# A decoder trunk's down projection by seven products per four blocks, woven into the up projection

## Chip, cores and metric

One Trainium2 chip, one core. The metric is the time of one execution on the device, in microseconds (us); the lower the better.

## The reference

One inference step of two decoder layers, d_model 1024, for 512 prompt tokens and 32 sample tokens (8 sequences of 4), which share all weights:

```python
x += W_out [ Retention(h) || DilatedAttention(h) ],  h = RMSNorm(x), one projection h @ W_in
x += ConvFFN(RMSNorm(x))

def conv_ffn(h, ctx, w_up_l, conv_w_l, conv_b_l, w_down_l):
    u = h @ w_up_l
    ext = concatenate([ctx, u], axis=1)
    c = conv_b_l
    for j in range(3):
        c = c + ext[:, j:j + T] * conv_w_l[j]
    g, val = c[..., :2816], c[..., 2816:]
    return (silu(g) * val) @ w_down_l, ext[:, -2:]
```

W_up is 1024 x 5632, W_down 2816 x 1024. The change leaves what is computed as it is.

## The kernel before

All activations lie with features on the 128 partitions and the 544 tokens along the free axis, as two halves of 272 (`HC`), each with 256 prompt and 16 sample tokens. x is eight tiles `x[n]`, one per 128 features.

**Products.** Every large product runs in three passes of split operands: a tile `t` is split into a high part (ACT copies it into the type fp32r) and a low part (DVE subtracts). Then high x high, high x low and low x high are summed in PSUM. `products` (line 1196) issues for one block of 128 rows of weights 3 passes x 2 halves = 6 matmuls of 272 columns. A main block (`add_block`, line 297) is one block of 128 output features: 8 such groups of 6 for an up block, 4 or 5 for a down block. Here one group of 6 is called a step. Main blocks go to a PSUM tile `ps` of two banks, of which there are two (`main_bank`, line 349). Weights arrive in halves of a block: `load_w` (line 306) issues a DMA into `raw` (six buffers) on SP's queue, six halves ahead; `split_w` (line 312) makes `wh` on ACT and `wl` on DVE, three halves ahead.

**Order.** Nothing is scheduled at run time. The program writes its instructions through `Engine` (line 94), whose `call` at line 112 is the line that every row of the profile names, so rows are told apart by their tiles. `Clock` keeps an estimated time for each engine; `Stream` (line 153) holds generators of side work (attention, conv, norms, splits) and, between two steps of main products, `pump` emits a piece of those whose operands should be ready by that estimate. Each engine then runs its own list in order. Smaller matmuls of side work go to four PSUM banks, `sec`.

**FFN** (`ffn`, line 1063). The 22 blocks of the hidden dimension are worked in groups of 5, 5, 4, 4, 4 (`GROUPS`, line 25). `add_up` puts for each j two up blocks (gate and value half); `conv` (line 1078) follows each: DVE scales `ps` into `u` (2 rows), POOL puts the context into u and copies the new context out, ACT and then DVE twice make the three-tap sum `c`, ACT applies silu to the gate's, DVE multiplies into `y` (2 rows), ACT and DVE split it into `yh` and `yl`. `add_down` puts eight main blocks per group, which multiply the group's `yh`, `yl` by W_down; `down` adds each result to `x[n]` on DVE. The order is up(0), up(1), down(0), up(2), down(1), ..., up(4), down(3), down(4). The last eight main blocks of the program run once per half of the tokens, so that their successive matmuls have other weights each time and one bank.

**Mixer** (`mixer`, line 882). 28 blocks of W_in with attention and retention as side work; POOL adds the two terms of the rotary embedding (`ka`, `qa`, `kr`, `qr`) and multiplies `qd`. Then eight blocks of W_out twice.

## Time and profile before

| | before |
|---|---|
| time, median of 3 runs | 1444.89 us (1444.69 to 1445.34) |
| the profiled execution's own time | 1444.82 us |
| its span, first to last instruction | 1443.0 us |
| mean granted clock of TensorE | 0.997 of full speed |
| busy PE, DVE, ACT, POOL | 99%, 66%, 40%, 12% of the span |
| mean DMA rate | 121 GB/s |

PE is TensorE's matmul, PEld its loading of weights, which overlaps; DVE is VectorE, ACT ScalarE, POOL GpSimd, SP the queue that issues all DMAs. In a time line the first number is the start in us from the span's start, the second the length, x2 two rows put together; a bracket gives the idle time before the row and what ended it. An instruction's length holds its tail, so two rows that follow each other overlap a little: the step from one start to the next is what a row costs its engine.

### The profile page before, as it was taken

Reading aid. Unit: us, or ns where it says so; the run is one execution under the profiler, and the core shown is the slowest. Engines: PE = TensorE matmul, PEld = TensorE weight load, DVE = VectorE, ACT = ScalarE, POOL = GpSimd, SP = SyncE. Lnnn points to the kernel's source line nnn. Section 1 sums busy time; section 2 is a strip of 40 time slices with the busy share of each in tenths; the row PEclk is TensorE's granted clock in tenths of the full one; section 3 lists DMA queues with packets and bytes.
Section 4 is the critical chain, followed back from the end, with each engine's and each line's share of the span. In section 5 each row is a group of like instructions: output and inputs, shape, how many; then the busy total and the mean of one; then the engine's idle time right before and its main releaser. Section 6 shows DMA issues by size and latency. Waiting matters only on the chain.

```text
span 1443.0 us, 29646 instructions
## 1 busy us (share of the span) xinstructions
PE 1423.1 (99%) x11634; PEld 1356.0 (94%) x11634; DVE 949.2 (66%) x1857; ACT 571.6 (40%) x1108; POOL 178.9 (12%) x553
## 2 busy tenths in 40 slices
PE   8999999999999999999999999999999999999997
PEld 8888788999999999999998878899999999999996
DVE  8876556588775565757678765566977647566665
ACT  4454333444443333424435442243444424333334
POOL 4212222000000000000022221120000000000003
PEclk9999999999999999999999999999999999999999
DMA  6315682433222222223322339722422232322231
GB/s 237 97 60 181 233 311 89 154 113 115 93 80 88 91 83 101 93 84 104 104 90 90 119 105 316 283 91 101 148 104 88 65 112 70 107 88 89 88 93 63
DMA packets 98635, 173.92 MB, mean 121 GB/s; under 512 B 11072, under 2 KB 21440, under 8 KB 98496
## 3 DMA queue, kind: packets, MB, share of 16 engines
q1 hardware_dynamic: 98496, 172.03, 35.3%
q8 instruction: 92, 1.51, 0.4%
q14 instruction: 47, 0.39, 0.1%
HBM read 159.77 MB, written 12.21 MB: 119 GB/s over the span
## 4 chain that ended last, share of the span: by engine, by line
PE 94%; DVE 3%; issue 1%; DMA 0%; ACT 0%; SPq 0%; DVEq 0%; POOL 0%; ACTq 0%
PE ps L112 82%; PE sec L112 12%; DVE wl L112 1%; DVE rb L112 1%; DMA x<-xin 0%; DVE p L112 0%; SPq L112 0%; DVE xl L112 0%; DVE ra L112 0%; DVE sq L112 0%; ACT xh L112 0%; DVE va L112 0%; POOL qa L112 0%; DVEq L1381 0%; DVE tmp L112 0%
## 5 line engine op out<-in xcount | busy, mean ns | idle before, releaser
L112 PE MATMUL ps<-xh,wh 128*128 128x272 f32 x2304 | 489.0, 294 | 1.4 <-ACT wh L112 1.1
L112 PE MATMUL ps<-xh,wl 128*128 128x272 f32 x2304 | 477.3, 289 | 0.7 <-DVE wl L112 0.7
L112 PE MATMUL ps<-xl,wh 128*128 128x272 f32 x2304 | 477.3, 289 | 0.0
L112 PEld LDWEIGHTS ps<-xh,wh 128*128 128x128 f32 x2304 | 361.2, 189 | 19.0 <-issue 14.7
L112 PEld LDWEIGHTS ps<-xh,wl 128*128 128x128 f32 x2304 | 362.3, 189 | 0.9 <-DVE wl L112 0.9
L112 PEld LDWEIGHTS ps<-xl,wh 128*128 128x128 f32 x2304 | 362.3, 189 | 0.0
L112 ACT ACTIVATE wh<-raw 128x512 fp32r<-128x512 f32 (+2 forms) x432 | 248.3, 598 | 172.0 <-PE ps L112 158.8
L112 DVE TENSOR_TENSOR wl<-raw,wh 128x512 fp32r<-128x512 f32 (+2 forms) x432 | 295.9, 703 | 18.7 <-ACT wh L112 17.9
L112 DVE SCALAR_TENSOR_TENSOR c<-u,taps,c 128x560 f32<-128x560 f32 x176 | 141.2, 802 | 89.0 <-ACT c L112 85.9
L112 ACT ACTIVATE c<-u,taps 128x560 f32<-128x560 f32 x88 | 75.5, 857 | 227.1 <-DVE u L112 223.7
L112 DVE TENSOR_TENSOR x<-x,ps 128x544 f32<-128x544 f32 (+1 forms) x120 | 81.7, 681 | 119.6 <-PE ps L112 119.2
L112 PE MATMUL ps<-yh,wh 128*128 128x272 f32 x704 | 150.9, 288 | 0.0
L112 PE MATMUL ps<-yh,wl 128*128 128x272 f32 x704 | 150.5, 288 | 0.0
L112 PE MATMUL ps<-yl,wh 128*128 128x272 f32 x704 | 150.4, 288 | 0.0
L112 DVE TENSOR_TENSOR u<-ps,rstd 128x512 f32<-128x512 f32 (+1 forms) x176 | 69.2, 435 | 80.5 <-PE ps L112 80.4
L112 PEld LDWEIGHTS ps<-yh,wh 128*128 128x128 f32 x704 | 112.3, 188 | 0.1
L112 PEld LDWEIGHTS ps<-yl,wh 128*128 128x128 f32 x704 | 112.2, 188 | 0.1
L112 PEld LDWEIGHTS ps<-yh,wl 128*128 128x128 f32 x704 | 112.3, 188 | 0.0
L112 POOL COPY last<-u 128x2 f32<-128x2 f32 (+1 forms) x176 | 28.2, 192 | 667.2 <-DVE u L112 630.3
L112 DVE TENSOR_TENSOR rb<-ps,rope 32x544 f32<-32x544 f32 (+1 forms) x96 | 69.2, 721 | 1.4
L112 ACT ACTIVATE yh<-y 128x544 fp32r<-128x544 f32 x44 | 29.0, 659 | 82.6 <-DVE y L112 82.6
L112 PE MATMUL ps<-ch,wh 128*128 128x272 f32 x256 | 53.4, 290 | 0.0
(147 smaller groups left out, 1343.3 us busy)
## 6 DMA issues: line engine op xcount, KB each, us to landing
raw<-w_up SPq DMA_DIRECT2D x176, 256.0 KB, 2.8
raw<-w_in SPq DMA_DIRECT2D x112, 256.0 KB, 3.9
kt<-kc SPq DMA_DIRECT2D x80, 256.0 KB, 5.2
vt<-vc SPq DMA_DIRECT2D x80, 256.0 KB, 5.2
raw<-w_down SPq DMA_DIRECT2D x48, 256.0 KB, 2.6
raw<-w_out SPq DMA_DIRECT2D x32, 256.0 KB, 2.7
raw<-w_down SPq DMA_DIRECT2D x32, 192.0 KB, 2.4
s<-s SPq DMA_DIRECT2D x16, 256.0 KB, 5.3
```

What stands on the lines that cost most here:

```text
L112: return f(*args, **kw)
```

## The change

Of the 22 hidden blocks the first 16, in four groups of four, are multiplied by W_down in another way; the groups are now 4, 4, 4, 4, 2, 4. A group's four blocks are taken as two pairs (a, b), and the eight output blocks as four pairs m. With the two halves of the tokens, each 2 x 2 block product of a pair takes seven products of half width instead of eight (Strassen's method in Winograd's form).

- `make_forms` takes the place of the split of y for these 16: per pair of blocks four subtractions of 272 on POOL (`fa`, `fb`), then splits into `hb`/`lb`, `h1`/`l1` and twice `fh`/`fl`.
- `Weave.prepare` loads for each m the four blocks of weights in one DMA (`uraw`, 512 KB), makes four sums on POOL (`sums`, 4 rows of 2 x 128) and splits (`ah`/`al` of 768, `sh`/`sl` twice 512). Each of these tiles has one buffer.
- `Weave.step` issues one of the products P1, P4, P6, P2, P5, P7, P3: 2 pairs x 3 passes = 6 matmuls of 272 columns into one `sec` bank. P1, P6, P5, P3 go on in one bank, which ACT copies out between them (`one`, `snap`); `after` adds the results to x[2m] and x[2m+1], on DVE (three rows of 272, one of 544) and POOL (one of 272, one of 544).
- `tick` runs after each step of the next group's up blocks, of which there are 64: from the 24th on it puts the 28 woven steps among the 40 that remain, a step when it is due and its operands should be ready by the estimate, at the latest so that all are through at the 64th.
- The groups of 2 and 4 at the end are multiplied as before. Weights are loaded and split by whole blocks of eight, or of two or four smaller blocks together (`shared`), three units ahead for the load and two for the split; 432 splits become 182. Some tiles of the mixer (`qpad`, `qdp`, `k3`, `v3`, `vs`, `vss`) take the buffers of the woven weights, and `bd` those of the pool of blocks.

```diff
-GROUPS = ((0, 5), (5, 10), (10, 14), (14, 18), (18, 22))
+GROUPS = ((0, 4), (4, 8), (8, 12), (12, 16), (16, 18), (18, 22))
+MP = KB // 2
+STEPS = (("P1", 0, 0), ("P4", 0, 2), ("P6", 1, 1), ("P2", 0, 1), ("P5", 1, 0), ("P7", 1, 2), ("P3", 1, 3))
+LEAD, AMONG = 24, 40
...
-    def add_block(src, nk, rhs, evac, pre=None):
+    def add_block(src, nk, rhs, evac, pre=None, weave=None, shared=(0, 1)):
         i = len(main)
-        parts = [(0, nk)] if nk <= 4 else [(0, (nk + 1) // 2), ((nk + 1) // 2, nk)]
...
+        at, count = shared
+        parts = [(0, nk)] if i > 1 else [(0, nk // 2), (nk // 2, nk)]
...
+        if at == 0:
+            for a, b in parts:
+                halves.append((i, a, a + count * (b - a)))
...
+    def make_forms(a, b, first, i, dst):
+        fa, fb = blk([128, 2, HC], F32, "fa"), blk([128, 2, HC], F32, "fb")
+        pool.tensor_sub(fa[:, 0], a[:, 1], a[:, 0])
+        pool.tensor_sub(fa[:, 1], b[:, 1], fa[:, 0])
+        pool.tensor_sub(fb[:, 0], b[:, 1], a[:, 1])
+        pool.tensor_sub(fb[:, 1], b[:, 0], fa[:, 1])
+        hb = blk([128, 2, HC], F32R, "hb")
+        act.activation(hb, b, AF.Copy)
+        act.activation(first[0][:, i], a[:, 0], AF.Copy)
+        yield EW("dve", first[0], hb)
+        lb = blk([128, 2, HC], F32R, "lb")
+        dve.tensor_sub(lb, b, hb.bitcast(F32))
+        dve.tensor_sub(first[1][:, i], a[:, 0], first[0][:, i].bitcast(F32))
+        dst["P1"] = first[0][:, i], first[1][:, i]
+        dst["P2"] = hb[:, 0], lb[:, 0]
+        dst["P3"] = hb[:, 1], lb[:, 1]
+        for f, one, two_ in ((fa, "P5", "P6"), (fb, "P7", "P4")):
+            yield EW("act", f)
+            h = blk([128, 2, HC], F32R, "fh")
+            act.activation(h, f, AF.Copy)
+            yield EW("dve", h)
+            l = blk([128, 2, HC], F32R, "fl")
+            dve.tensor_sub(l, f, h.bitcast(F32))
+            dst[one] = h[:, 0], l[:, 0]
+            dst[two_] = h[:, 1], l[:, 1]
...
+    class Weave:
...
+        def tick(self):
+            self.count += 1
+            if not self.todo:
+                return
+            left = len(self.todo)
+            if self.count >= LEAD + (7 * MP - left) * AMONG / (7 * MP):
+                if self.count + left >= LEAD + AMONG or self.ready(*self.todo[0]):
+                    self.step(*self.todo.pop(0))
+                    if not self.todo:
+                        self.end()
+
+        def ready(self, m, p, g, q):
+            if (m, g) not in self.weights or any(p not in self.forms(i) for i in range(self.nk)):
+                return False
+            aps = [*self.weights[m, g], *(t for i in range(self.nk) for t in self.forms(i)[p])]
+            return clock.when("pe", aps) <= clock.now["pe"]
+
+        def prepare(self):
+            for m in range(MP):
+                w = wpool.tile([128, self.nk, 4, 128], F32, name=name("uraw"), tag="uraw", bufs=1)
+                sp.dma_start(w, self.src[m])
+                yield EW("pool", w)
+                sums = wpool.tile([128, self.nk, 4, 128], F32, name=name("sums"), tag="sums", bufs=1)
+                pool.tensor_add(sums[:, :, 0], w[:, :, 3], w[:, :, 2])
+                pool.tensor_sub(sums[:, :, 1], sums[:, :, 0], w[:, :, 0])
+                yield EW("pool", w)
+                pool.tensor_sub(sums[:, :, 2], w[:, :, 0], w[:, :, 3])
+                pool.tensor_sub(sums[:, :, 3], w[:, :, 1], sums[:, :, 1])
+                yield IF(lambda: m == 0 or (m - 1, "P2") in self.seen)
+                yield EW("act", w)
+                ah, al = (wpool.tile([128, self.nk, 3, 128], F32R, name=name(n), tag=n, bufs=1) for n in ("ah", "al"))
+                act.activation(ah, w[:, :, 0:3], AF.Copy)
+                yield EW("dve", ah)
+                dve.tensor_sub(al, w[:, :, 0:3], ah.bitcast(F32))
+                self.weights[m, 0] = ah, al
+                yield IF(lambda: m == 0 or (m - 1, "P3") in self.seen)
+                sh, sl = (wpool.tile([128, self.nk, 4, 128], F32R, name=name(n), tag=n, bufs=1) for n in ("sh", "sl"))
+                for a in (slice(0, 2), slice(2, 4)):
+                    yield EW("act", sums)
+                    act.activation(sh[:, :, a], sums[:, :, a], AF.Copy)
+                    yield EW("dve", sh)
+                    dve.tensor_sub(sl[:, :, a], sums[:, :, a], sh[:, :, a].bitcast(F32))
+                self.weights[m, 1] = sh, sl
+
+        def step(self, m, p, g, q):
...
+            for i in range(self.nk):
+                st.until(lambda: p in self.forms(i))
+                r = self.forms(i)[p]
+                st.before([*w, *r])
+                for j, (wi, ri) in enumerate(passes):
+                    pe.matmul(bank[:, :HC], lhsT=w[wi][:, i, q, :], rhs=r[ri],
+                              start=before is None and i == 0 and j == 0, stop=i == self.nk - 1 and j == 2,
+                              skip_group_check=True)
+            self.seen.add((m, p))
+            st.spawn(self.after(m, p, bank[:, :HC], self.snaps), "snap",
+                     EW("act" if p in ("P1", "P6", "P5") else "dve", bank))
+            st.pump(0.7)
+
+        def after(self, m, p, bank, snaps):
+            x1, x2 = x[2 * m], x[2 * m + 1]
+            self.seen.add((m, "read " + p))
+            if p == "P1":
+                one = blk([128, HC], F32, "one")
+                act.activation(one, bank, AF.Copy)
+                yield EW("pool", one)
+                pool.tensor_add(x1[:, 0], x1[:, 0], one)
+                self.seen.add((m, "one"))
+            elif p == "P4":
+                yield EW("dve", x2)
+                dve.tensor_add(x2[:, 0], x2[:, 0], bank)
+                done()
+            elif p == "P6":
+                act.activation(snaps[:, 0], bank, AF.Copy)
+            elif p == "P2":
+                yield IF(lambda: (m, "one") in self.seen)
+                yield EW("dve", x1)
+                dve.tensor_add(x1[:, 0], x1[:, 0], bank)
+                done()
+            elif p == "P5":
+                act.activation(snaps[:, 1], bank, AF.Copy)
+                yield IF(lambda: (m, "x2") in self.seen)
+                yield EW("pool", snaps, x2)
+                pool.tensor_add(x2, x2, snaps)
+            elif p == "P7":
+                yield EW("dve", x2)
+                dve.tensor_add(x2, x2, bank[:, None, :].to_broadcast([128, 2, HC]))
+                done()
+                self.seen.add((m, "x2"))
+            elif p == "P3":
+                yield EW("dve", x1)
+                dve.tensor_add(x1[:, 1], x1[:, 1], bank)
+                done()
 
...
+        def forms():
+            for gi in range(ended):
+                yield IF(lambda: F.ready >= gi)
+                a, b = GROUPS[gi]
+                first = [blk([128, 2, HC], F32R, n) for n in ("h1", "l1")]
+                for i, j in enumerate(range(a, b, 2)):
+                    yield IF(lambda: j in F.raw and j + 1 in F.raw)
+                    yield EW("pool", F.raw[j], F.raw[j + 1])
+                    dst = F.forms[gi, i] = {}
+                    yield from make_forms(F.raw.pop(j), F.raw.pop(j + 1), first, i, dst)
+
+        def woven(gi):
+            a, b = GROUPS[gi]
+
+            def end():
+                F.ready = gi + 1
+                for i in range((b - a) // 2):
+                    F.forms.pop((gi, i))
+            return Weave([q_down[l, m, :, a // 2:b // 2] for m in range(MP)], (b - a) // 2,
+                         lambda i: F.forms.get((gi, i), {}), end)
 
         def begin():
             st.spawn(norm.finish(), "norm")
+            st.spawn(forms(), "form")
...
+            if j < GROUPS[ended][0]:
+                F.raw[j] = y
+                return
...
+        weave = None
+        for gi, (a, b) in enumerate(GROUPS):
+            if 0 < gi <= ended:
+                weave = woven(gi - 1)
+            for j in range(a, b):
+                pre = begin if j == 0 else weave.start if weave and j == a and gi <= ended else None
+                add_block(w_up[l, j], KB, rhs, up(0, j), pre=pre, weave=weave)
+                add_block(w_up[l, FB + j], KB, rhs, up(1, j), weave=weave)
+        a, b = GROUPS[ended]
+        for n in range(KB):
+            add_block(w_down[l, n - n % 4:n - n % 4 + 4, :, a:b, :], b - a, lambda k, a=a: F.y[a + k], down(n, False),
+                      shared=(n % 4, 4))
+        a, b = GROUPS[-1]
+        for n in range(KB):
+            add_block(w_down[l, n, :, a:b, :], b - a, lambda k, a=a: F.y[a + k], down(n, True),
+                      pre=(lambda: st.drain("ffn")) if n == 0 else None)
...
-            load_w(s + 6)
-            split_w(s + 3)
-            w = parts_of(s)
-            split.pop(s)
+            at, count = b["at"], b["count"]
+            if at == 0:
+                load_w(s + 3)
+                w = parts_of(s)
+                split.pop(s)
             for k in range(a, e):
-                products(b, ps, k, w, a)
+                if 2 * (at * (e - a) + k - a) == count * (e - a):
+                    split_w(s + 2)
+                products(b, ps, k, w, a - at * (e - a))
                 st.pump(0.7)
+                if b["weave"]:
+                    b["weave"].tick()
```

**PE, first FFN, where the second woven group begins.** Before, an up block (`ps_5656`, operands xh, xl) is followed by a whole down block (`yh`, `yl`):

```order
L112 MATMUL ps_5656<-xh_4200,wh_5580 128x272 x2
L112 MATMUL ps_5656<-xl_4216,wh_5580 128x272 x2
L112 MATMUL ps_5656<-xh_4200,wl_5581 128x272 x2
L112 MATMUL ps_5729<-yh_4448,wh_5612 128x272 x2
L112 MATMUL ps_5729<-yl_4488,wh_5612 128x272 x2
L112 MATMUL ps_5729<-yh_4448,wl_5613 128x272 x2
```

Now P4 of the first pair of output blocks (`sec_5765`) stands between two up blocks:

```order
L118 MATMUL ps_5690<-xh_3995,wh_5548 128x272 x2
L118 MATMUL ps_5690<-xl_4010,wh_5548 128x272 x2
L118 MATMUL ps_5690<-xh_3995,wl_5549 128x272 x2
L118 MATMUL sec_5765<-fh_5546,ah_5589 128x272
L118 MATMUL sec_5765<-fl_5557,ah_5589 128x272
L118 MATMUL sec_5765<-fh_5546,al_5590 128x272
L118 MATMUL sec_5765<-fh_5721,ah_5589 128x272
L118 MATMUL sec_5765<-fl_5741,ah_5589 128x272
L118 MATMUL sec_5765<-fh_5721,al_5590 128x272
L118 MATMUL ps_5782<-xh_3707,wh_5635 128x272 x2
L118 MATMUL ps_5782<-xl_3720,wh_5635 128x272 x2
L118 MATMUL ps_5782<-xh_3707,wl_5636 128x272 x2
```

The down block's products have moved in among the up steps. P1 of this pair stands 8 up steps ahead of P4, after `ps_5601`. In the order of both layers P4 is 2 up steps behind P1 in the first group, 8 in the second and third and 9 in the fourth; in the second and third the steps of the first two pairs after that, and in the fourth those of nearly all, stand one up step apart.

**DVE, the same place: the end of the stretch in which P4's operand `fl_5741` is made.** Before, a stretch of conv rows with two splits per up block:

```order
L112 TENSOR_TENSOR u_4504<-ps_4436,rstd_4249 128x512
L112 TENSOR_TENSOR u_4504<-ps_4436,rstd_4249 128x8x4
L112 SCALAR_TENSOR_TENSOR c_4509<-u_4504,taps,c_4509 128x560 x2
L112 TENSOR_TENSOR wl_4517<-raw_4391,wh_4516 128x512
L112 TENSOR_TENSOR wl_4549<-raw_4437,wh_4548 128x512
L112 TENSOR_TENSOR y_4564<-c_4432,c_4509 128x2x256
L112 TENSOR_TENSOR y_4564<-c_4432,c_4509 128x2x16
L112 TENSOR_TENSOR u_4579<-ps_4513,rstd_4249 128x512
L112 TENSOR_TENSOR u_4579<-ps_4513,rstd_4249 128x8x4
L112 SCALAR_TENSOR_TENSOR c_4584<-u_4579,taps,c_4584 128x560 x2
```

Now:

```order
L118 TENSOR_TENSOR al_5590<-uraw_5436,ah_5589 128x768
L118 SCALAR_TENSOR_TENSOR c_5597<-u_5592,taps,c_5597 128x560 x2
L118 TENSOR_TENSOR wl_5636<-raw_5516,wh_5635 128x1024
L118 TENSOR_TENSOR y_5668<-c_5511,c_5597 128x2x256
L118 TENSOR_TENSOR y_5668<-c_5511,c_5597 128x2x16
L118 TENSOR_TENSOR u_5681<-ps_5601,rstd_4033 128x512
L118 TENSOR_TENSOR u_5681<-ps_5601,rstd_4033 128x8x4
L118 TENSOR_TENSOR fl_5706<-fa_5559,fh_5658 128x544
L118 TENSOR_TENSOR sl_5634<-sums_5496,sh_5633 128x2x256
L118 SCALAR_TENSOR_TENSOR c_5686<-u_5681,taps,c_5686 128x560 x2
L118 TENSOR_TENSOR fl_5741<-fb_5560,fh_5721 128x544
L118 TENSOR_TENSOR sl_5634<-sums_5496,sh_5633 128x2x256
```

The last up block's conv rows (`u`, `c`) now stand among `al`, `sl` and the two `fl`; `fl_5741` is the eleventh row. From `u_5418`, the first row after the preceding group's last up block, to `fl_5741` the list has four u, four times two c, two lb, four fl, two l, two y, three wl of 1024, one al and one sl.

**POOL, the same place.** Before, POOL has only the four small rows of each up block:

```order
L112 MEMSET u_6151 128x2
L112 COPY u_6151<-ctx_4171 128x8x2
L112 COPY last_4173<-u_6151 128x2
L112 COPY last_4173<-u_6151 128x16
L112 MEMSET u_6224 128x2
```

Now the forms of the second pair (`fa_5559`, `fb_5560`) come behind the sums and these rows:

```order
L118 TENSOR_TENSOR sums_5496<-uraw_5436 128x2x128
L118 TENSOR_TENSOR sums_5496<-sums_5496,uraw_5436 128x2x128
L118 MEMSET u_5506 128x2
L118 COPY u_5506<-ctx_3967 128x8x2
L118 COPY last_3969<-u_5506 128x2
L118 COPY last_3969<-u_5506 128x16
L118 TENSOR_TENSOR sums_5496<-uraw_5436 128x2x128
L118 TENSOR_TENSOR sums_5496<-uraw_5436,sums_5496 128x2x128
L118 TENSOR_TENSOR fa_5559<-y_5233 128x272
L118 TENSOR_TENSOR fa_5559<-y_5487,fa_5559 128x272
L118 TENSOR_TENSOR fb_5560<-y_5487,y_5233 128x272
L118 TENSOR_TENSOR fb_5560<-y_5487,fa_5559 128x272
```

Between `u_5418` and `fl_5741` POOL has eight rows of forms, four of sums and one addition to x, besides the small rows.

## Rows read from the trace of the kernel before

**Rows 1.** The page: span, then busy time, its share and instructions of each engine.
```profile
span 1443.0 us, 29646 instructions
PE 1423.1 (99%) x11634; PEld 1356.0 (94%) x11634; DVE 949.2 (66%) x1857; ACT 571.6 (40%) x1108; POOL 178.9 (12%) x553
```

**Rows 2.** Busy time by stage: both FFN stretches, then pieces of both mixers.
```profile
core 0: us, PE busy (x) PEld busy (x) DVE busy (x) ACT busy (x) POOL busy (x), PEclk, DMA share, GB/s
333.20:724.60 391.40, 391.40 (x3128) 391.40 (x3127) 254.13 (x442) 153.54 (x249) 22.60 (x175) 1.00 0.29 93
1041.30:1418.00 376.70, 376.70 (x3002) 376.70 (x3001) 238.08 (x421) 145.97 (x242) 25.55 (x179) 1.00 0.27 89
20.00:60.00 40.00, 37.89 (x292) 35.67 (x291) 37.78 (x67) 12.67 (x32) 13.75 (x16) 1.00 0.36 125
746.00:850.00 104.00, 102.84 (x830) 89.23 (x829) 77.28 (x188) 47.50 (x135) 24.22 (x32) 1.00 0.32 109
```

**Rows 3.** The chain in order of time: start, us, what, count of instructions.
```profile
333.21 391.43 PE ps L112 x3126
...
1041.32 376.76 PE ps L112 x3000
1420.21 11.39 PE ps L112 x90
```

**Rows 4.** Time line of DVE at the head of the second FFN: start, us, instruction.
```profile
1041.60 0.78 DVE L112 TENSOR_TENSOR u<-ps,rstd 128x512 f32<-128x512 f32 x2
1042.30 0.68 DVE L112 SCALAR_TENSOR_TENSOR s<-s,sec 128x512 f32<-128x512 f32 x1
1043.37 1.64 DVE L112 SCALAR_TENSOR_TENSOR c<-u,taps,c 128x560 f32<-128x560 f32 x2 [0.39 <-ACT c L112]
1044.92 0.69 DVE L112 TENSOR_TENSOR wl<-raw,wh 128x512 fp32r<-128x512 f32 x1
...
1049.80 0.80 DVE L112 TENSOR_TENSOR y<-c,c 128x512 f32<-128x512 f32 x2 [0.27 <-ACT c L112]
1050.51 0.69 DVE L112 TENSOR_TENSOR wl<-raw,wh 128x512 fp32r<-128x512 f32 x1
1051.12 0.79 DVE L112 TENSOR_TENSOR u<-ps,rstd 128x512 f32<-128x512 f32 x2
...
1055.03 0.72 DVE L112 TENSOR_TENSOR yl<-y,yh 128x544 fp32r<-128x544 f32 x1
1055.67 0.69 DVE L112 TENSOR_TENSOR wl<-raw,wh 128x512 fp32r<-128x512 f32 x1
```

**Rows 5.** Time line of DVE in the last products.
```profile
1410.60 0.44 DVE L112 TENSOR_TENSOR x<-x,ps 128x272 f32<-128x272 f32 x1 [0.44 <-PE ps L112]
1410.96 0.69 DVE L112 TENSOR_TENSOR wl<-raw,wh 128x512 fp32r<-128x512 f32 x1
```

**Rows 6.** Time line of ACT at the head of the second FFN.
```profile
1042.48 0.86 ACT L112 ACTIVATE c<-u,taps 128x560 f32<-128x560 f32 x1 [3.88 <-DVE u L112]
1043.24 0.62 ACT L112 ACTIVATE wh<-raw 128x512 fp32r<-128x512 f32 x1
```

**Rows 7.** Time line of POOL in the last products (one of five alike).
```profile
1410.08 0.77 POOL L112 TENSOR_TENSOR sq<-sq,sq 128x272 f32<-128x272 f32 x1 [26.82 <-ACT sq L112]
```

**Rows 8.** Time line of POOL in the first mixer.
```profile
210.63 1.50 POOL L112 TENSOR_TENSOR qr<-ra,rb 128x512 f32<-128x512 f32 x2 [6.25 <-PE ps L112]
212.08 1.29 POOL L112 TENSOR_TENSOR qd<-qr,cst 128x512 f32<-128x512 f32 x1
```

**Rows 9.** Time line of DVE in the same stretch.
```profile
211.00 0.69 DVE L112 CUSTOM_DVE_ANT_0 sp<-sec,cst 128x512 f32<-128x512 f32 x1 [0.51 <-PE sec L112]
...
212.14 1.78 DVE L112 TENSOR_TENSOR wl<-raw,wh 128x512 fp32r<-128x512 f32 x1
213.84 0.68 DVE L112 TENSOR_TENSOR sm<-sec,cst 128x512 f32<-128x512 f32 x1
```

**Rows 10.** Time line of DVE beside POOL's ka, which began at 35.09 us.
```profile
35.04 2.40 DVE L112 TENSOR_TENSOR wl<-raw,wh 128x512 fp32r<-128x512 f32 x2
```

**Rows 11.** PE's waits: us in total, times, longest.
```profile
PE sec L112 <- DVE p L112: 5.0, 4, 1.8
```

**Rows 12.** DMA issues: count, KB each, median us from issue to landing.
```profile
raw<-w_up SPq DMA_DIRECT2D x176, 256.0 KB, 2.8
```

**Rows 13.** Time line of PE in the first products, then a window's granted clock.
```profile
8.28 0.52 PE L112 MATMUL ps<-xh,wh 128*128 128x272 f32 x2 [1.12 <-ACT wh L112]
8.63 0.41 PE L112 MATMUL ps<-xl,wh 128*128 128x272 f32 x2
9.76 0.52 PE L112 MATMUL ps<-xh,wl 128*128 128x272 f32 x2 [0.72 <-DVE wl L112]
...
10.88 0.66 PE L112 MATMUL ps<-xh,wl 128*128 128x272 f32 x2
11.33 0.66 PE L112 MATMUL ps<-xh,wh 128*128 128x272 f32 x2
...
10.00:12.00 2.00, 2.00 (x11) 2.00 (x11) 2.00 (x2) 1.90 (x4) 1.92 (x2) 0.57 1.05 409
```

More of the change, by code (lines that the diff above doesn't have):

```diff
@@ L895, in begin @@
             rope_tables(L, l, 2)()
-            L.qpad = work.tile([128, 4, NB, 32], F32, name=name("qpad"), tag="qpad", bufs=1)
+            L.qpad = lent([128, 4, NB, 32], F32, "sh")
             pool.memset(L.qpad, 0.0)
             L.ks = small([128, 4, 32], "ks", 1)
-            L.vs = small([32, 512], "vs", 1)
+            L.vs = lent([32, 512], F32, "uraw")
             L.os = small([128, 4, NB, T], "os", 1)
@@ L938, in start_ret @@
         def start_ret():
-            L.qdp = work.tile([128, 4, NB, 32], F32, name=name("qdp"), tag="qpad2", bufs=1)
+            L.qdp = lent([128, 4, NB, 32], F32, "sl")
             pool.memset(L.qdp, 0.0)
-            L.k3 = work.tile([96, 4, 128], F32R, name=name("k3"), tag="k3", bufs=1)
-            L.v3 = work.tile([96, 4, 128], F32R, name=name("v3"), tag="v3", bufs=1)
-            L.vss = small([32, 4, 128], "vss", 1)
+            L.k3 = lent([96, 4, 128], F32R, "ah")
+            L.v3 = lent([96, 4, 128], F32R, "al")
+            L.vss = lent([32, 4, 128], F32, "sums")
             L.sts = small([32, 4, 32], "sts", 1)
```

105 lines of the change are left out of this document (62 added, 43 removed).

## Prediction

> **What bounds the kernel now.** I read the page's busy shares first, then busy time by stage, then the chain of waits, then time lines of the engines the change loads. The page shows the matmul engine (PE) busy for 1423.1 of 1443.0 us and everything else far below [rows 1]. By stage, the two FFN stretches have no idle PE time at all at a granted clock of 1.00, with DVE at 65% and 63%, ACT at 39%, POOL at 6 to 7% and the DMA engines under 30% [rows 2]. The chain says the same: one unbroken piece of PE work of 391.43 us with 3126 matmuls, and one of 376.76 us with 3000 [rows 3]. That is 0.1254 us a matmul on average. In FFN only fewer matmuls can help, and anything that makes PE wait costs in full. The last twelve or so microseconds show the pace when successive matmuls have other weights and the same bank, as the new steps have: 11.39 us for 90, 0.1266 [rows 3]. So a woven step is as cheap per matmul as the products it replaces.
>
> **What goes.** Of each layer's 22 down blocks of 128 rows 16 go through seven half-width products per four blocks: 4 groups x 4 pairs x 7 x 2 x 3 = 672 matmuls where 16 x 8 x 6 = 768 stood. The listing has 192 fewer of 272 columns over both layers: 192 x 0.1254 = **24.1 us less**.
>
> **What comes.** Before any of it is a cost, the durations. Where DVE's rows follow each other the next one starts after 0.70 us (u, both parts), 1.55 (the two c rows), 0.71 (y, both parts), 0.61 (wl of 512), 0.64 (yl of 544) [rows 4] and 0.36 (x of 272) [rows 5]. Per element that is 1.04 ns, so 0.88 for al, 1.14 for a whole block's wl. A c row starts 1.77 us after its u row, since ACT's c of 0.86 us lies between [rows 4, 6].
>
> POOL gets 256 new rows: forms (64), sums of weights (128), additions to x (64). A POOL row of 272 takes 0.77 us [rows 7], one of 512 takes 1.29 [rows 8], so one of 256 about 0.735. They are not free for DVE. At 212.14 us a wl of 512 took 1.78 us while POOL's qd ran from 212.08 for 1.29; the next DVE row began 1.70 after it instead of 0.61 after it, so qd cost DVE 1.09, or 0.85 of its duration. At 211.00 a DVE row that reads PSUM and one SBUF tile took 0.69 beside a POOL row and lost nothing [rows 8, 9]. Two wl beside POOL's ka took 2.40 in place of 1.3 [rows 10]. So rows with two SBUF operands (c, y, wl, al, sl, fl, lb) and POOL rows take turns, and u and x rows don't take part. The Trainium skill's page "SBUF — State Buffer" ("SBUF: two separate sides") has the same rule in a harder form: a DVE op with two SBUF inputs and a GpSimd op that reads SBUF hold their shared ports for the whole instruction and the other fully blocks. By whole durations the sum below would be 1457 us, by the measured 0.85 it is 1441; rows 8 and 9 speak for slightly less than the whole.
>
> **Where it meets PE.** In the second, third and fourth group of each layer P4 stands 8 or 9 up steps after P1, as the pieces of order show, and its second half needs fl from fb of the group's second pair. Counting from the end of the preceding up block, PE gets there after 24 steps, P1, 8 steps and half of P4: (24 x 6 + 6 + 8 x 6 + 3) x 0.1254 = 25.2 us. DVE has in that stretch four u, four pairs of c, two lb, four fl, two l, two y, three wl, one al and one sl: 2.8 + 6.2 + 1.3 + 2.6 + 0.7 + 1.4 + 3.4 + 0.9 + 0.6 = 19.9 us, and waits of 1.07 (for the first c) and 1.20 (for an up block that ends at 12.04): done after 22.2, so 3.0 us early. POOL has 13 rows there, eight forms, four sums and one x: at 0.85 of their durations 8 x 0.65 + 4 x 0.62 + 0.65 = 8.3 us. Bounds: if they fall on u rows and waits (5.1 us of the 22.2), 3.2 is paid and the wait of 1.20 swallows part of it: no PE wait. If all is paid, 22.2 + 8.3 - 1.2 = 29.3: **4.1 us late**; by whole durations (9.9) 5.7. With the two-operand rows' share of the stretch, 17.1 of 22.2, 6.4 is paid: 2.2 late. Both queues are full there as they are in rows 10, where every POOL row was paid, so I take the middle of 2.2 and 4.1, **3.1 us**, six times: 18.6 us. In each layer's first group P4 follows P1 after 2 steps and one pair's forms were made during the group before; there I count nothing, 6 us at most.
>
> After P4 the seven steps of a pair of output blocks come at one up step each in the tight places: 14 x 6 x 0.1254 = 10.5 us. DVE needs 7/8 of an up block (0.70 + 1.55 + 0.36 + 1.14 = 3.75) = 3.3, and al, two sl, three x of 272 and one of 544 = 3.8: 7.1. POOL's four sums and two additions are worth 4.3 at most: 11.4 against 10.5, so 0 to 0.9 a pair, 14 such pairs, 0 to 12.6. PE's wait at P4 has just let DVE catch up: 0.3 a group, **2.4 us**.
>
> The next costs are small. Each step of a running bank waits for ACT's copy of it; P4 or a like step and two up steps lie between (18 matmuls, 2.3 us) and even a 0.86 us row fits: nothing, or 1 us now and then within the bound just given. SP gets one issue of 512 KB per pair in place of two or more smaller ones; the weight bytes stay and DMA is below 30% [rows 2]: nothing. Splitting whole blocks makes one wl of 1.14 out of two; in the mixer a POOL row now catches one row where it caught two, but attention's short DVE rows may queue behind a longer one. PE idles there 2.1 us in 20 to 60 and 1.2 in 746 to 850 [rows 2], which bounds the gain at 3.3; its four waits on p, 5.0 us together [rows 11], could grow by 0.53 each: +2.1. Taken: **-1.0**. In the last eight blocks the loads run three ahead instead of six: a transfer of 2.8 us [rows 12] and a split of 0.62 (no more on ACT than on DVE) + 0.61 over three buffers make 1.35 us a block, against 12 x 0.1266 = 1.5: **0.5**, 0 to 2. The conv rows of the last up blocks lose half of their cover, but 96 matmuls, 12 us, stay over a chain of about 6: nothing.
>
> **Sum.** -24.1 + 18.6 + 2.4 - 1.0 + 0.5 = -3.6. Against the profiled execution's own 1444.82 us (span 1443.0 and 1.8 around it; the median of the runs is 1444.89, the same) that is **1441.2 us**. What a measurement of this kernel can tell from no change is 0.2%, 2.9 us.
>
> **Rivals.**
> POOL hides. Its rows fall beside u and x rows and DVE's waits; no wait at P4: 1444.8 - 24.1 + 2.4 - 1.0 + 0.5 = 1422.6. For it: DVE idles a third of FFN today [rows 2]. Against it: the stretch before P4 has 19.9 us of work in 22.2.
> The port decides (slower). Every POOL row is paid with its whole duration, DVE has fl 5.7 us late, PE stands at P4 six times: 34.2 in place of 18.6, 1456.8. It decides from 3.7 us each, (24.1 - 2.4 + 1.0 - 0.5) / 6. Waits that long may also cost clock: after PE's waits of 1.12 and 0.72 us near 8 us the granted clock was 0.57 for some 4 us and pairs of matmuls came 0.45 apart instead of 0.25 [rows 13], 1.8 us lost; six times that gives 1467.6. This is the skill's rule of the shared ports at its word.
> The weights bind. P4 as forecast, but each tight pair pays its 0.9: 12.6 in place of 2.4, 1451.4. For it: al, sl and sums have one buffer each. Against it: DVE has just caught up.
>
> **How the numbers follow.** Forecast 0.42, from 1436 (2.2 us late) to 1447 (4.1): within it faster 0.22, same 0.15, slower 0.05. POOL hides 0.28, port 0.20, weights 0.10. So faster 0.50, same 0.15, slower 0.35. The range runs from the first rival's 1422 to 1462, between the port rival without and with a lower clock. The forecast's own range is 1436 to 1447.
>
> **What would show it.** Right: 192 fewer matmuls at 0.125; idle PE time in FFN ahead of sec<-fl or fh, released by DVE fl, six times 2 to 4 us; al, sl, fl and wl longer than 0.9, 0.6, 0.6 and 1.1 us; DVE above 80% in FFN. Wrong: no such PE waits (POOL hid), PE waits chiefly on sl, al or an up block's u (weights, or DVE full throughout), or a granted clock under 1.00 in FFN.

## The result and the profile after

The changed kernel takes **1453.43 us** (median of 4 runs, 1453.17 to 1454.0) against 1445.12 for the kernel before beside it: a ratio of 1.0052, interval 1.0039 to 1.0065. It is slower by half a per cent; forecast were 1441.2 us and, with a chance of 0.5, faster. The time lies within the range from 1422 to 1462, but outside the forecast's own from 1436 to 1447, and on the other side of no change.

The page of the changed kernel: span, busy time, then the chain's shares by engine and line, then groups (busy us, mean ns, idle before and its releaser).

```profile
span 1452.0 us, 28531 instructions
...
PE 1406.9 (97%) x11442; PEld 1332.6 (92%) x11442; DVE 1056.4 (73%) x1815; ACT 612.1 (42%) x1082; POOL 489.3 (34%) x809
...
PE 69%; DVE 19%; issue 5%; POOL 4%; ACT 2%; DMA 0%; SPq 0%; DVEq 0%; ACTq 0%; POOLq 0%
...
L118 DVE SCALAR_TENSOR_TENSOR c<-u,taps,c 128x560 f32<-128x560 f32 x176 | 159.0, 903 | 73.7 <-ACT c L118 70.5
...
L118 POOL TENSOR_TENSOR x<-x,snap 128x544 f32<-128x544 f32 x32 | 54.7, 1708 | 144.1 <-DVE x L118 139.5
...
L118 POOL TENSOR_TENSOR sums<-uraw 128x256 f32<-128x256 f32 x64 | 60.1, 940 | 38.9 <-DVE sl L118 30.7
...
L118 DVE TENSOR_TENSOR sl<-sums,sh 128x512 fp32r<-128x512 f32 x64 | 64.8, 1029 | 1.5 <-ACT sh L118 1.5
```

PE is busy 16.2 us less than in [rows 1], while the span is 9.0 longer: PE waits now. DVE has gone from 949.2 to 1056.4 us, POOL from 178.9 to 489.3. c took 802 ns on DVE on the page of before and takes 903.

Busy time by stage. A stage begins with its first product of x (ps<-xh) in the PE time line: first mixer, first FFN, second mixer, second FFN with the tail. The kernel before:

```profile
core 0: us, PE busy (x) PEld busy (x) DVE busy (x) ACT busy (x) POOL busy (x), PEclk, DMA share, GB/s
0.00:322.40 322.40, 315.22 (x2647) 281.98 (x2647) 220.51 (x478) 133.71 (x300) 66.74 (x103) 0.99 0.48 165
322.40:720.75 398.35, 398.35 (x3178) 398.06 (x3177) 260.54 (x452) 155.62 (x254) 22.60 (x175) 1.00 0.29 93
720.75:1030.52 309.77, 306.86 (x2628) 274.67 (x2627) 206.64 (x465) 122.98 (x284) 56.27 (x91) 1.00 0.44 151
1030.52:1443.00 412.48, 402.72 (x3189) 401.26 (x3187) 261.52 (x462) 159.34 (x272) 33.29 (x184) 0.99 0.27 89
```
The changed kernel, the same four stages:

```profile
0.00:324.91 324.91, 316.05 (x2649) 282.19 (x2649) 215.00 (x446) 129.51 (x264) 65.63 (x103) 0.99 0.47 164
324.91:725.68 400.77, 390.04 (x3079) 386.82 (x3078) 319.35 (x462) 179.91 (x276) 178.84 (x304) 1.00 0.27 91
725.68:1038.90 313.22, 308.40 (x2630) 275.56 (x2629) 201.34 (x433) 118.60 (x248) 54.67 (x91) 1.00 0.43 151
1038.90:1452.00 413.10, 392.44 (x3091) 388.07 (x3089) 320.70 (x474) 184.12 (x296) 190.12 (x313) 0.99 0.26 89
```

The first column behind the stage is its length. The mixers are 2.5 and 3.5 us longer, where a gain of 1.0 was forecast; the FFN stretches 2.4 and 0.6, where 96 matmuls fewer in each should have given 12.0. So FFN lost 27.1 us, the mixers 6.0, and 24.1 were gained: +9.0, as the spans say. The granted clock in the first FFN stretch is still 1.00.

What PE waited for in the first FFN stretch (total us, times, longest; `snap` and `one` are ACT's copies of the running bank):

```profile
PE sec L118 <- ACT snap L118: 4.1, 4, 1.6
PE sec L118 <- DVE al L118: 2.9, 3, 1.1
PE sec L118 <- DVE fl L118: 2.1, 3, 0.8
PE sec L118 <- ACT one L118: 1.1, 1, 1.1
PE sec L118 <- DVE sl L118: 0.3, 1, 0.3
PE ps L118 <- ACT yh L118: 0.3, 1, 0.3
```

That is 10.8 us. The idle time shown is too small for each wait: a matmul row lasts 0.29 us but the next may start 0.125 after it, so the first 0.16 us of a wait look busy. Counted from start to start in the time line the same stretch loses about 3.4 us at al (P1), 2.5 at fl (P4) and 6.0 at ACT's copies of the running bank (four waits on `snap`, one on `one`), and the second 3.5, 2.2 and 6.1. P4's wait on fl, which was to be 3.1 us, is 0.7 to 0.9.

One of the longest waits, at 478.23 us, in the changed kernel's time line of PE (start, us, instruction, idle time before it and its releaser):

```profile
478.23 0.39 PE L118 MATMUL sec<-fh,sh 128*128 128x272 f32 x1 [1.60 <-ACT snap L118]
```

Its time line of ACT there:

```profile
477.04 0.85 ACT L118 ACTIVATE c<-u,taps 128x560 f32<-128x560 f32 x1 [4.69 <-POOL u L118]
477.80 0.38 ACT L118 ACTIVATE snap<-sec 128x272 f32<-128x272 f32 x1
```

Of DVE:

```profile
477.93 1.64 DVE L118 SCALAR_TENSOR_TENSOR c<-u,taps,c 128x560 f32<-128x560 f32 x2 [2.86 <-ACT c L118]
```

Of POOL, up to the copy into u:

```profile
472.96 1.66 POOL L118 TENSOR_TENSOR sums<-uraw 128x256 f32<-128x256 f32 x1 [1.92 <-DVE sl L118]
474.70 0.74 POOL L118 TENSOR_TENSOR sums<-sums,uraw 128x256 f32<-128x256 f32 x1
475.40 0.74 POOL L118 TENSOR_TENSOR sums<-uraw 128x256 f32<-128x256 f32 x1
476.10 0.73 POOL L118 TENSOR_TENSOR sums<-uraw,sums 128x256 f32<-128x256 f32 x1
...
476.81 0.20 POOL L118 COPY u<-ctx 128x16 f32<-128x16 f32 x1
```

Read from the top, the chain goes back through all four engines. P5 waits 1.60 us for `snap`, ACT's copy of the bank after P6. ACT has long been free, but `snap` stands behind c of an up block, and c waited 4.69 us for POOL: for the copy of 16 context columns into u (0.20 us), which stands behind four rows of sums. DVE, 80% busy in this stretch, idles 2.86 us for the same c. The sums were late too: POOL idled 1.92 us before them until DVE's sl had read the old ones, since sums has one buffer. In the kernel before no c waited for POOL.

### The profile page after: what moved, and what is told of

Read it like the earlier page. It is cut to its first block, busy times and chain, and to the rows that moved or that the text cites. A ratio compares the mean times of both kernels' runs of the same rounds, so it can differ in the third digit from the quotient of the medians.

```text
span 1452.0 us, 28531 instructions
## 1 busy us (share of the span) xinstructions
PE 1406.9 (97%) x11442; PEld 1332.6 (92%) x11442; DVE 1056.4 (73%) x1815; ACT 612.1 (42%) x1082; POOL 489.3 (34%) x809
## 4 chain that ended last, share of the span: by engine, by line
PE 69%; DVE 19%; issue 5%; POOL 4%; ACT 2%; DMA 0%; SPq 0%; DVEq 0%; ACTq 0%; POOLq 0%
PE ps L118 48%; PE sec L118 20%; DVE wl L118 3%; DVE c L118 3%; DVE p L118 3%; DVE rb L118 2%; POOL sums L118 2%; DVE u L118 2%; DVE y L118 1%; ACT c L118 1%; DVE sl L118 1%; DVE ra L118 1%; DVE fl L118 1%; DVE l L118 1%; DVE al L118 1%
## 5 line engine op out<-in xcount | busy, mean ns | idle before, releaser
L118 DVE TENSOR_TENSOR wl<-raw,wh 128x1024 fp32r<-128x1024 f32 (+1 forms) x182 | 219.0, 1204 | 27.2 <-ACT wh L118 26.6
L118 ACT ACTIVATE wh<-raw 128x1024 fp32r<-128x1024 f32 (+1 forms) x182 | 182.2, 1002 | 67.3 <-PE ps L118 59.0
L118 POOL TENSOR_TENSOR x<-x,snap 128x544 f32<-128x544 f32 x32 | 54.7, 1708 | 144.1 <-DVE x L118 139.5
L118 DVE TENSOR_TENSOR x<-x,sec 128x272 f32<-128x272 f32 (+1 forms) x128 | 63.6, 500 | 27.1 <-POOL x L118 22.6
L118 POOL TENSOR_TENSOR sums<-uraw 128x256 f32<-128x256 f32 x64 | 60.1, 940 | 38.9 <-DVE sl L118 30.7
L118 DVE TENSOR_TENSOR x<-x,ps 128x544 f32<-128x544 f32 (+1 forms) x72 | 46.9, 654 | 31.3 <-PE ps L118 31.2
L118 DVE CUSTOM_DVE_ANT_0 p<-sec,cst 128x128 f32<-128x128 f32 (+3 forms) x64 | 29.2, 489 | 53.4 <-PE sec L118 53.1
L118 DVE TENSOR_TENSOR sl<-sums,sh 128x512 fp32r<-128x512 f32 x64 | 64.8, 1029 | 1.5 <-ACT sh L118 1.5
L118 PE MATMUL sec<-fh,sh 128*128 128x272 f32 x192 | 56.1, 292 | 9.7 <-ACT snap L118 7.5
L118 PE MATMUL sec<-fh,sl 128*128 128x272 f32 x192 | 55.5, 289 | 0.3 <-DVE sl L118 0.3
```

What stands on the lines that cost most here:

```text
L118: return f(*args, **kw)
```

## The experiments

Two theories were put against each other for the FFN's loss. **Q, the queue:** short POOL rows that an up block needs stand behind the new long ones, and ACT's bank copies behind the c that waits for them. **P, the port:** POOL rows that read SBUF make DVE's two-operand rows long, and PE waits on what DVE delivers late. For the mixers' loss there is **W**, the weights' split by whole blocks, against **L**, the lent buffers. The times are medians; ratios are to the kernel before, run beside each on the same chip. Its median was 1445.1 us beside the changed kernel and 1446.3 to 1446.7 beside the others, so 0.1% between the changed kernel's ratio and theirs is not told apart. Stages are cut as above, from one profiled execution of each kernel.

| kernel | us | ratio, interval | mixer 1 | FFN 1 | mixer 2 | FFN 2 + tail |
|---|---|---|---|---|---|---|
| before | 1445.1 | 1 | 322.4 | 398.4 | 309.8 | 412.5 |
| changed | 1453.4 | 1.0052 [1.0039, 1.0065] | 324.9 | 400.8 | 313.2 | 413.1 |
| e1 early edges | 1444.3 | 0.9985 [0.9976, 0.9994] | 325.1 | 395.6 | 312.8 | 409.0 |
| e2 constants | 1438.3 | 0.9941 [0.9927, 0.9954] | 325.3 | 392.8 | 313.2 | 405.5 |
| e3 whole units alone | 1449.2 | 1.0017 [1.0008, 1.0026] | 324.9 | 398.3 | 312.8 | 411.0 |
| e4 half units | 1501.1 | 1.0375 [1.0361, 1.0389] | 322.8 | 424.8 | 310.1 | 440.2 |
| e5 = e1 + mixers by halves | 1443.5 | 0.9980 [0.9971, 0.9989] | 324.7 | 396.4 | 311.6 | 408.6 |
| e6 = e5, later steps | 1444.8 | 0.9990 [0.9981, 0.9999] | 325.6 | 396.8 | 311.6 | 409.6 |
| e7 = e1 + e2 | 1429.0 | 0.9881 [0.9866, 0.9896] | 324.7 | 388.0 | 313.1 | 401.3 |
| e8 = e5, forms on DVE | 1443.2 | 0.9977 [0.9968, 0.9986] | 325.3 | 396.1 | 311.5 | 409.0 |
| e9 = e5, both on DVE | 1436.1 | 0.9927 [0.9913, 0.9940] | 325.2 | 392.1 | 312.0 | 405.2 |
| e10 = e5, sums on DVE | 1443.8 | 0.9981 [0.9972, 0.9990] | 324.9 | 396.0 | 311.9 | 409.0 |
| e11 = e9, splits placed as before | 1432.5 | 0.9908 [0.9893, 0.9923] | 324.7 | 391.7 | 309.9 | 404.8 |
| e12 = e11, without early edges | 1432.6 | 0.9903 [0.9887, 0.9920] | 322.8 | 391.5 | 311.6 | 404.8 |

**e1, the queue alone.** The order of PE, DVE, ACT and SP stays; 88 pairs of POOL rows move forward by a block.

```diff
+        def edge(s, j):
+            if (s, j) not in F.u:
+                u = F.u[s, j] = blk([128, BLK], F32, "u")
+                us = u[:, 514:562].rearrange("p (b j) -> p b j", j=6)
+                nc.gpsimd.memset(u[:, 0:2], 0.0)
+                nc.gpsimd.tensor_copy(us[:, :, 0:2], F.ctx[s][:, j])
...
-                add_block(w_up[l, FB + j], KB, rhs, up(1, j), weave=weave)
+                add_block(w_up[l, FB + j], KB, rhs, up(1, j), pre=lambda j=j: edge(1, j), weave=weave)
```

> The changed kernel with 88 pairs of short POOL rows (the memset and the copy of the context columns into u) put one up block earlier in POOL's order, and nothing else moved on any engine. Theory Q (POOL's queue: these rows stand behind the new sums, forms and x rows, ACT's c waits for them, 16 of 44 times in each FFN stretch and 54 us together, and ACT's copies of the running bank, ah and sh stand behind c): those 16 waits go, PE's idle time in each FFN stretch falls from 10.7 us to under 5, and the time is about 1440 us (1433 to 1445). Rival P (the shared port: POOL's rows make DVE's two-operand rows long, and everything is late by that): c stays at 0.90 us on DVE, PE's waits stay, the time is 1450 to 1455.

What ACT's c waited for in the changed kernel (whole span; total us, times, longest):

```profile
ACT c L118 <- DVE u L118: 171.2, 54, 5.6
ACT c L118 <- POOL u L118: 109.2, 32, 5.0
```

And in e1:

```profile
ACT c L118 <- DVE u L118: 240.3, 80, 5.6
```

The 32 waits on POOL's u are gone, and with them 9 us, all in FFN. Q is shown, at the weak end of what was expected of it: PE still idles about 6.5 us in the first FFN stretch where under 5 was expected, mostly at al and fl, over the program six times about 1.0 and six times about 0.8 us. That c stays at 0.90 us on DVE was P's claim, and it came true as well.

**e2, the port alone.** POOL writes constants for about as long, in the same place.

```diff
+    def filled(out, times, whole, *ins):
+        pool.charge("tensor_sub", [out], list(ins), (), {})
+        for _ in range(times):
+            nc.gpsimd.memset(whole, 0.01)
...
-        pool.tensor_sub(fa[:, 0], a[:, 1], a[:, 0])
+        filled(fa[:, 0], 2, fa, a[:, 1], a[:, 0])
...
-                pool.tensor_add(sums[:, :, 0], w[:, :, 3], w[:, :, 2])
+                filled(sums[:, :, 0], 1, sums, w[:, :, 3], w[:, :, 2])
```

> The changed kernel with POOL's forms and sums left out: in their places POOL writes a constant (memset), two of 544 elements for each form row and one of 1024 for each sums row, so that POOL is about as long busy in the same order but reads nothing there. Rival P (port): DVE's c falls from 0.90 to 0.80 us, wl from 1.20 to 1.12, sl from 1.03 to 0.65, PE's waits in the FFN stretches go with them, the time is about 1437 us (1432 to 1442). Theory Q (queue): DVE's rows get shorter as well, but ACT's c still waits for POOL's copy into u, and the time stays above 1446 us.

One place of the program in the changed kernel, the time line of DVE:

```profile
459.86 1.81 DVE L118 TENSOR_TENSOR wl<-raw,wh 128x1024 fp32r<-128x1024 f32 x1
```

And of POOL:

```profile
458.18 1.16 POOL L118 TENSOR_TENSOR fa<-y,fa 128x272 f32<-128x272 f32 x1
459.30 1.29 POOL L118 TENSOR_TENSOR fb<-y,y 128x272 f32<-128x272 f32 x1
460.54 1.76 POOL L118 TENSOR_TENSOR fb<-y,fa 128x272 f32<-128x272 f32 x1
```

The same place in e2, the time line of DVE:

```profile
456.33 1.22 DVE L118 TENSOR_TENSOR wl<-raw,wh 128x1024 fp32r<-128x1024 f32 x1
```

And of POOL:

```profile
455.31 1.78 POOL L553 MEMSET fa<- 128x544 f32 x3
457.04 2.38 POOL L553 MEMSET fb<- 128x544 f32 x4
```

wl of 1024 elements takes 1.81 us beside POOL's fb rows and 1.22 beside constants. In the first FFN stretch of e2 every DVE row of wl, al, sl, fl, lb or c that is longer than alone lies beside an addition to x, or a rotary row at its head; none is long for a constant. P is shown as well, and its 1437 was right: 1438.3. DVE, with the same rows in the same order, is busy 1014.3 us in place of 1056.4. What PE waits for in the first FFN stretch of e2:

```profile
PE sec L118 <- ACT snap L118: 4.1, 5, 1.4
PE ps L118 <- ACT yh L118: 0.3, 1, 0.3
```

The waits on al and fl are gone. Q's claim that the waits on POOL's u would hold the time above 1446 was not right: 38 such waits remain, 138 us of ACT's time, and PE still meets ten waits on ACT's copies in the program, 7.9 us in place of 10.4, but al and fl, which had cost another 9.7, no longer hold it. One thing e2 changes besides: POOL no longer waits for y and for the loads of uraw, 6.1 us of its idle time in the changed kernel's first FFN stretch; this was not tested apart. What was expected of sl fell too: its mean stayed at 1025 ns, since its long rows lie beside the additions to x, which e2 keeps. The Trainium skill, "SBUF — State Buffer", section "SBUF: two separate sides", has the pair of ports locked against a DVE op with two SBUF inputs only by a GpSimd op that reads SBUF; these rows agree.

**e7, both cures.** The edit is e1's and e2's together.

> The second experiment's kernel (POOL writes constants in place of the forms and the sums, which it leaves out) with the edges of u written early as well: what the port costs once POOL's queue holds nothing up. If the two causes add (queue 9 us, port 15 us below the changed kernel's 1453.4): about 1429 us. If they are one chain of delays (either cure takes the same waits away): 1434 to 1438, little under the second experiment's 1438.3.

1429.0: the two add. FFN falls to 388.0 us, 10.4 below before, and PE's waits there are 0.4 for a snap and 0.2 for yh. Over both stretches e7 wins back 24.7 of the 27.1 us, so nearly all of FFN's loss is POOL's work, through its queue and through its port.

**e3 and e4, the size of the units.** e3 puts whole-block units into the kernel before; e4 puts half-block units into the changed one.

```diff
-        parts = [(0, nk)] if nk <= 4 else [(0, (nk + 1) // 2), ((nk + 1) // 2, nk)]
+        at, count = shared
+        parts = [(0, nk)] if i > 1 else [(0, nk // 2), (nk // 2, nk)]
...
-            load_w(s + 6)
-            split_w(s + 3)
+            if at == 0:
+                load_w(s + 3)
...
+                if at * (e - a) + k - a == half:
+                    split_w(s + 2)
```

> The kernel before with one part of the change alone: weights loaded and split by whole blocks (three buffers of 8 blocks of 128 rows each for raw, wh and wl, the split halfway through a block), no Strassen products, no lent buffers. Theory W (whole-block splits make the mixers longer: the changed kernel's two mixer stretches are 2.5 and 3.4 us longer than before's, an up or input block's wl of 1.14 us now stands in one piece ahead of attention's DVE rows): about 1450 us (1448 to 1453), all of it in the mixers. Rival L (the mixers are longer because their tiles were moved to lent buffers and to the pool of blk): 1443 to 1446.

> The changed kernel with the weights loaded and split by half blocks as before (raw 6, wh and wl 5 buffers of 4), the Strassen steps, lent buffers and the rest kept. Theory W: the mixers fall back by 5 to 6 us, the FFN stretches stay: about 1448 us (1446 to 1450). Rival L: the mixers stay, 1452 to 1455.

With the table's stages this is a square of four kernels. The mixers go with the units alone: 322.4 and 309.8 or 322.8 and 310.1 by halves, 324.9 and 313.2 or 324.9 and 312.8 by whole blocks. W holds, L falls. PE's waits in the second mixer of the kernel before on `p`, a tile of attention that DVE makes:

```profile
PE sec L112 <- DVE p L112: 2.5, 2, 1.7
```

And of e3, on `p` and on `pm`, a small tile that goes with it:

```profile
PE sec L113 <- DVE p L113: 3.5, 4, 1.1
PE sec L113 <- DVE pm L113: 0.7, 2, 0.4
```

For FFN the expectation of e4 was far off: with the Strassen steps half units cost 24 and 27 us more; without them whole units change nothing in the first stretch and save 1.5 us in the second. Half units mean more DVE rows, the order that `Stream` writes moves (P1 comes some ten up steps later, and P4 then only two or three after it instead of eight or nine), and P4 meets the kind of wait that had been forecast. The second of them in e4's time line of PE:

```profile
480.33 0.60 PE L118 MATMUL sec<-fl,ah 128*128 128x272 f32 x1 [5.14 <-DVE fl L118]
```

And the stretches around it in e4 (busy time by engine, then the granted clock):

```profile
465.00:475.00 10.00, 9.59 (x76) 9.28 (x74) 9.93 (x14) 6.60 (x13) 8.88 (x11) 1.00 0.38 128
475.00:482.00 7.00, 1.86 (x8) 1.67 (x8) 5.72 (x7) 0.27 (x1) 5.26 (x6) 0.78 0.00 0
482.00:495.00 13.00, 13.00 (x91) 12.85 (x90) 6.91 (x11) 5.65 (x10) 2.00 (x3) 0.85 0.26 82
```

5.14 us at fl, eight such waits and 29.8 us over the program, besides 14.0 us on sl, and a granted clock of 0.85 over the 13 us behind it. So the forecast's mechanism and the port rival's lower clock both exist; with whole units, and the order that comes with them, the change escapes them. Whether by the fewer DVE rows or by the order was not separated. The change had bought its FFN relief with the mixers.

**e5 and e11, the mixers.** e5 loads whole blocks for w_in and w_out but splits them in two halves within one block; e11, on top of e9, puts the halves where the kernel before has them (the edit from e9 to e11):

```diff
-                n8 = 8 * (at * (e - a) + k - a) // (count * (e - a))
-                ahead = s + 2 < len(halves) and main[halves[s + 2][0]]["fine"]
-                if n8 in ((2, 6) if ahead else (4,)) and 8 * (at * (e - a) + k - a) % (count * (e - a)) == 0:
-                    split_w(s + 2, part=n8 // 6 if ahead else None)
+                if at == 0 and k == a and s + 1 in begun and s + 1 not in split:
+                    split_w(s + 1, part=1)
+                if 2 * (at * (e - a) + k - a) == count * (e - a):
+                    fine2 = s + 2 < len(halves) and main[halves[s + 2][0]]["fine"]
+                    split_w(s + 2, part=0 if fine2 else None)
```

> The first experiment's kernel (edges of u written early), with the weights of the mixers' blocks (w_in, w_out) still loaded as whole blocks but split by halves, two ACT rows and two DVE rows of 512 elements at a quarter and at three quarters of a block; FFN's blocks as changed, whole. Theory W (the one piece of 1.22 us on DVE costs the mixers 2.5 and 3.2 us): the mixers fall back to 322.5 and 310 us, the FFN stretches stay at 395.6 and 409.0, about 1438.7 us (1437 to 1441). Rival (the mixers pay for the later loads of whole blocks, three in flight instead of six): the mixers stay at 325 and 313, 1443 to 1445.

> The kernel of the ninth experiment (edges early, forms and sums on DVE, mixers' weights loaded whole and split by halves, 1436.1 us) with the two halves of a mixer block split where the kernel before splits them: the first half in the middle of the block two ahead of it, the second at the start of the block just ahead, instead of both within one block. Rival to W, now W2 (not the length of the DVE piece but the place of the splits among attention's rows sets what is left of the mixers' loss, 2.8 and 2.2 us): mixers 322.8 and 310.1 us, about 1431.5 us. If loads of 512 KB three ahead are the cause: 1435 to 1437, the mixers as in the ninth experiment.

e5 missed: 0.4 and 1.2 us came back of 2.7 and 3.0, so the length of one DVE piece is the smaller part. In e11 PE's waits on p are two in each mixer again, as before, and its second mixer takes 309.9 us; the first of e12, with the same order in the mixers, 322.8. Those are before's lengths, with loads of 512 KB three ahead: the place of the splits among attention's rows is most of what the whole units cost. The other mixer of each is 1.7 to 1.9 us longer for another reason, the granted clock, the third figure from the right: part of each such stretch ran at half of full speed. In e11's first mixer:

```profile
146.00:156.00 10.00, 8.26 (x74) 6.33 (x73) 5.08 (x10) 4.36 (x12) 4.32 (x11) 0.83 0.12 29
```

In e12's first mixer and at the same wait of its second:

```profile
146.00:156.00 10.00, 8.27 (x87) 6.62 (x86) 5.44 (x13) 3.98 (x11) 3.95 (x10) 1.00 0.11 28
851.00:857.00 6.00, 6.00 (x53) 4.54 (x55) 1.57 (x5) 3.03 (x9) 0.74 (x5) 0.72 0.01 3
```

**e6, the steps later.**

```diff
-LEAD, AMONG = 24, 40
+LEAD, AMONG = 26, 38
...
-            return clock.when("pe", aps) <= clock.now["pe"]
+            return clock.when("pe", aps) + 1.0 <= clock.now["pe"]
```

> The kernel of the run before it in this call, with the first step of a group two up steps later (LEAD 26, AMONG 38 in place of 24 and 40) and a step taken early only if its operands are ready by the model 1.0 us before. Theory T (timing: the six waits on al at P1 of 1.0 us and the six on fl at P4 of 0.8 are single late rows, not a full DVE): they go, and nothing comes in their place; 5 to 9 us less than the run before it, about 1431 us. Rival F (DVE at 80% is full in a group: the steps are denser after a later start, and PE waits on sl, snap or al further on): within 3 us of the run before it, or slower.

The waits on al go, but fl takes 6.9 us where it took 4.4, and snap, one and sl 5.8 where they took 2.3. The rival's forecast holds: a wait that is dodged comes back at the next step. That DVE is full by its busy share alone is not the reason: e9 below has it at 86% of the first FFN stretch against 82% in e6, and PE's waits on fl are gone.

**e8, e9, e10 and e12: the rows moved to DVE.** In `make_forms` and `prepare` the eight lines `pool.tensor_sub` and `pool.tensor_add` become `dve.`; e8 has the forms alone, e10 the sums alone, e9 both, e12 both without e1's edit.

> The kernel of the fifth experiment (edges early, mixers split by halves, 1443.5 us) with the four forms of each pair of y blocks made by DVE instead of POOL: 64 DVE rows of 272 more at 0.36 us (23 us), 64 POOL rows fewer, which took 1.23 us each beside DVE. The port's price by this study: each such POOL row delays a DVE row by up to its own 0.75. If the port is what is left (15 us over 192 POOL rows, forms and sums): the forms' third and the four serial POOL rows ahead of fl go, DVE's busy time falls or stays, about 1437 us (1434 to 1440). Rival F (DVE full): no better, 1443 to 1447.

> The kernel of the fifth experiment with both forms and sums made by DVE, 192 rows more there (64 of 0.36 and 128 of about 0.34 us: 67 us), and only the additions to x left on POOL. Port: nothing of the 15 us is left but DVE has 67 - 47 = 20 us more to do than now, 1.3% of the span: about 1436 us (1432 to 1441). Rival F (DVE full): waits on sl and fl, 1445 or more.

> The kernel of the fifth experiment with the sums alone moved to DVE (128 rows, 44 us), the forms on POOL. Port: about 1440 us, less than the fifth by the sums' share of the port's cost and more than the eighth, since the serial forms ahead of fl stay. Rival F (DVE full): 1445 or more.

> The kernel beside it in this call without the early edges: the short POOL rows of u stand where the change leaves them, but POOL's queue now holds only the additions to x (64 rows) besides them. Theory Q: POOL's rows ahead of them are few, 0 to 3 us slower than the run beside it; ACT's c waits for POOL's u in fewer than 10 places instead of 32. If the additions to x, which wait for DVE's x, hold the queue as much as forms and sums did: 6 to 9 us slower.

Busy time in e9:

```profile
PE 1406.8 (98%) x11442; PEld 1334.5 (93%) x11442; DVE 1105.3 (77%) x2077; ACT 621.5 (43%) x1152; POOL 291.5 (20%) x617
```

e9 is as expected, 1436.1. e8 and e10 are not: neither gains anything over e5 (1443.2 and 1443.8 against 1443.5), though DVE is 1089 and 1110 us busy in them and 1105 in e9. With forms on DVE PE waits 7.0 us on snap and 2.6 on fl; with sums there, 7.5 on l and 2.3 on fl; with both, snap is 0.7 and fl and l are gone, with 3.5 on `one` left. Why half of the move gives nothing and the whole 7.4 us stays open: part of it may be the order, which `Stream` writes anew each time. In the second and third group P4 stands 8 up steps after P1 in e5, 4 in e8, 11 in e10 and 1 in e9, where P1 itself comes 7 up steps later. So e9 does not show what the move alone is worth. e12 says that the early edges are no longer needed once POOL holds only the additions to x. e11 and e12 are the fastest here that compute all of the reference, 0.9% below the kernel before.

## Why the prediction was wrong

- **192 matmuls fewer at 0.1254 us, -24.1:** right. The table's FFN stretches hold them, and in e7, with POOL out of the way, they are 10.4 and 11.2 us shorter than before's.
- **P4 late by fl, 3.1 us six times, +18.6:** right in kind, too large. Part of the lateness falls on P1 already, which waits on al; P1 and P4 together lose 1.9 us a group from start to start, 11.6 in place of 18.6, below the 2.2 that the text had by the two-operand rows' share. The prediction had P1 ready. The term that was too large is what POOL's thirteen rows take from DVE there: it was put at 6.4 to 8.3 us, but the time lines of DVE, row by row against the shortest of each kind, show 5.2 to 5.4 in each of the six groups. POOL's thirteen rows take 13.8 to 14.9 us there, where they would take 9.9 alone: POOL pays for the collisions about as much as DVE, and the prediction had charged them all to DVE.
- **The steps of the running bank, "nothing, or 1 us now and then", and the seven steps of a pair, 2.4:** this is a step that failed. ACT's copies were weighed against ACT's own rows and against DVE. They cost 12.1 us in ten waits, because c, which stands ahead of them, waits for POOL: 9.0 of the 12.1 go in e1, where it no longer does. The prediction counted what POOL's rows take from DVE and did not ask what stands behind them in POOL's own queue: in each up block a copy of 0.20 us, for which c waits. The bound of 12.6 held the size, the value taken did not.
- **Whole blocks in the mixers, -1.0:** the other step that failed. Both bounds were given (a gain of 3.3, a loss of 2.1), but the text took the gain for the POOL row that meets one piece instead of two. Measured are +6.0, beyond the bound of the loss. The four waits on p, the only rows named for a loss, became eight, and two on pm came in each mixer; e11 and e12 show that the place of the splits, which the text did not look at, is most of it.
- **The tail, +0.5:** not there. From the first to the last start, the 192 matmuls of the last eight blocks take 25.4 us in the kernel before and 25.3 in the changed one. The 1.5 us by which e3's second FFN is shorter lie ahead of these blocks and stay unexplained.
- **The sum.** -24.1 + 11.6 + 12.1 + 6.0 and 3.4 for small waits and what the time lines don't show one by one give +9.0. Of the error of 12.6 us against -3.6, the mixers are 7.0 and FFN 5.6: either of the two alone at its measured value would have taken the gain away.
- **The rivals.** "The port decides" gave 1456.8, for a wait at P4 that isn't there; its lower clock came only in e4. "The weights bind" gave 1451.4 and is the nearest number, partly by luck: it had 18.6 at P4 where 11.6 came, no loss in the mixers, and its 12.6 after P4 on al, sl and sums, where 12.1 came on ACT's copies. Of the three tiles it named, al is one of PE's waits, though at P1, sl hardly, and the one buffer of sums stands in the chain at 478 us; a second buffer was not tried. The text's own sign of being wrong, PE waiting on sl, al or an up block's u, came true in part.
